# Each subtraction that makes the low part of a weight chunk goes to GpSimd in two halves

## The chip, the cores and the metric

The kernel runs on one core of one Trainium2 chip. The time is device microseconds (us) of one execution, the median of the runs shown. Engines are named as in the profile: PE (TensorE matmul) and PEld (its weight loads), DVE (VectorE), ACT (ScalarE), POOL (GpSimd), SP (SyncE, which issues most DMAs).

## The reference, cut to what matters

Two layers of a diffusion backbone over 256 latent and 256 context tokens, width 1024, all in float32. A layer is a SwiGLU feed-forward (FFN), a mixer with three branches (gated linear attention, 2-D neighbourhood attention, grouped-query attention) that are gated and merged, and a second FFN. After the mixer of layer 1 only the 256 latent tokens go on.

```python
for l in range(DEPTH):
    ...
    x = x + 0.5 * g1 * swiglu(modulate(rms_norm(x, norm_g[l, 0]), sh1, sc1), ffn_w_in[l, 0], ffn_w_out[l, 0])
    h = h + 0.5 * cg1 * swiglu(modulate(rms_norm(h, norm_g[l, 0]), ch1, cs1), ffn_w_in[l, 0], ffn_w_out[l, 0])
    y, yc = token_mixer(...)
    x = x + g2 * y
    x = x + 0.5 * g3 * swiglu(modulate(rms_norm(x, norm_g[l, 2]), sh3, sc3), ffn_w_in[l, 1], ffn_w_out[l, 1])
    if need_ctx:
        ...
```

## The kernel before

The large products keep float32 accuracy with three passes of the faster fp32r form. Each operand is split into a high part (the value rounded to fp32r) and a low part (the value less its high part), and `mm3` issues high x high, high x low and low x high into one PSUM bank.

Weights come in 504 chunks. A chunk is 128 partitions by 1024 floats at most: four row blocks of 128 input rows by 256 columns (names `up`, `dn` and `pf` on PE), or two row blocks by 512 columns (`pt`); 16 `dn` chunks have two row blocks of 256 columns. The first index of a chunk's tile, `a` in the code, counts the row blocks. A chunk goes through four steps: a DMA into `w_raw` (three buffers), ACT's rounding copy into `w_hi`, POOL's subtraction `w_raw - w_hi` into `w_lo`, and the matmuls. `w_hi` and `w_lo` have three buffers each, so the split of a chunk starts only when PE has ended the chunk three places earlier. On a full chunk PE runs 24 matmuls for each stretch of tokens that it handles at a time (512 or 256 columns).

The order of all engines' instructions is fixed when the program is built. `Program.run` walks through the chunks; the main matmuls are issued directly, and side work (norms, attention heads, the modulation products `mod_acc`, the splits of chunks) stands in generators which are resumed after each few matmuls and which issue an instruction when a planner's clock (`Clock`) says that its inputs are there. The planner's durations decide the order only. For POOL it counts 0.1 us and 2.35 ns an element for each instruction, and it keeps the times of a tile's pieces apart.

At the start of a FFN or a mixer the two first column blocks are handled together (the `both` case in `ffn`, `proj_f2` in the mixer): one chunk is kept until its partner is there, and PE then goes through both, 256 tokens after 256 tokens. The activations `u_hi` and `u_lo` that these products read are made just then by a chain of DVE instructions (`norm_chain`).

In `splitter` the subtraction is one instruction of the whole chunk, except for four chunks at the very start (`halves`, set in `ffn` for the first FFN's first column blocks), where it is two instructions over half the row blocks each.

Of the kernel before, what the change touches and what calls it, by code (L numbers as in the profile page):

```python
# [49 lines left out]
def r32(ap):  # L50
    return ap.bitcast(F32R)
# [149 lines left out]
class Program:  # L201
# [76 lines left out]
        while self.urgent:  # L278
            self.round_or_stall()

    def chunk(self, src, a, b, fn, split=True, halves=False, kept=False):

        self.items.append(("c", (src, a, b, split, halves), fn))
        if kept:
            self.kept.add(sum(it[0] == "c" for it in self.items))

# [68 lines left out]
    def run(self):  # L355
        specs = [it[1] for it in self.items if it[0] == "c"]
        raws, parts, ended = {}, {}, {}
        state = {"loaded": 0, "ci": 0}

        def load(n):  # L360
            while state["loaded"] < min(len(specs), n):
                j = state["loaded"]
                src, a, b = specs[j][:3]
                raw = self.rpool.tile([P, a, b], F32, name="w_raw", tag="r", padded_shape=[P, 1024 // b, b])
                old = raws.get(j - RAW_BUFS)
                if old is not None:
                    self.clock.floor[raw.name] = self.clock.read.get(old.name, 0.0)
                self.clock.dma(raw)
                self.nc.sync.dma_start(raw, src)
                raws[j] = raw  # L370
                state["loaded"] += 1

        def splitter():
            for j, (src, a, b, do, halves) in enumerate(specs):
                while j > state["ci"] + SPLIT_AHEAD or (j >= SPLIT_BUFS and j - SPLIT_BUFS not in ended):
                    yield None
                load(j + 1)
                hi = self.wpool.tile([P, a, b], F32, name="w_hi", tag="w", padded_shape=[P, 1024 // b, b])
                lo = self.wpool.tile([P, a, b], F32, name="w_lo", tag="w", padded_shape=[P, 1024 // b, b])
                self.clock.floor[hi.name] = self.clock.floor[lo.name] = ended.get(j - SPLIT_BUFS, 0.0)  # L380
                raw = raws[j]
                yield from self.gact.copy(r32(hi), raw)
                h = a // 2 if halves else a
                for s in range(0, a, h):
                    yield from self.ggp.tensor_tensor(r32(lo[:, s : s + h]), raw[:, s : s + h], hi[:, s : s + h], op=ALU.subtract)
                parts[j] = (r32(hi), r32(lo))
                load(j + 1 + RAW_BUFS)
                if self.force:
                    yield None

        self.load = load
        split = splitter()

        def advance(g):

            self.first = True
            self._resume(g)
            self.first = False

        work = self.round  # L400

        def round_with_splits():
            n = self.clock.count
            advance(split)
            w = list(self.wakes)
            more = work()
            self.wakes += w
            return more or self.clock.count > n

        self.round = round_with_splits  # L410
        for kind, _, fn in self.items:
            if kind == "f":
                self.flush()
                fn()
                continue
            ci = state["ci"]
            load(ci + 1)
            self.force = True
            while ci not in parts:
                advance(split)  # L420
            self.force = False
            fn(parts.pop(ci))
            if ci + 1 not in self.kept:
                ended[ci] = self.clock.now
            if ci in self.kept:
                ended[ci - 1] = self.clock.now
            state["ci"] = ci + 1
        self.flush()
        assert not self.sides, list(self.sides)
# [3 lines left out]
def tile_backbone(ctx: ExitStack, tc: tile.TileContext, I: dict, out: bass.AP):  # L433
# [12 lines left out]
    prog = Program(nc, rpool, wpool)  # L446
# [22 lines left out]
    def acc_bank(name):  # L469
        t = psa.tile([P, 512], F32, name=name, tag="a")  # L470
        accs.append(t)
        if len(accs) > 4:
            clock.floor[t.name] = clock.read.get(accs[-5].name, 0.0)
        return t
# [183 lines left out]
    def lead(k, r):  # L658

        if k < 6 and k % 2 == 0:  # L660
            first_mm(k // 2 + 1, r)
        elif k % 2 and k < 7 and r == 0:
            first_u(k // 2 + 1)
# [167 lines left out]
    def need(r, k):  # L831

        while st["done"][r] <= k:
            prog.round_or_stall()
# [55 lines left out]
    def wsrc(w, k0, k1, c0, c1):  # L890
        return w[k0 * P : k1 * P, c0:c1].rearrange("(k p) n -> p k n", p=P)

    def ffn(l, i, which, n, square, ahead=(), lead=None):

        w_up, w_dn = I["ffn_w_in"][l, which], I["ffn_w_out"][l, which]
# [3 lines left out]
        def up(mp, part, kh, both=False):  # L899


            def fn(w):
                if both and part == 0:
                    hold["w"] = w
                    return
                ws = [(0, hold["w"]), (1, w)] if both else [(part, w)]
                for p, _ in ws:
                    if kh == 0:
                        hold[p] = [acc_bank("up") for _ in range(2)]
                parts = [slice(r, r + LAT) for r in range(0, n, LAT)] if both else [slice(0, n)]  # L910
                order = [(kk, r) for r in range(len(parts)) for kk in range(4)]
                for kk, r in sorted(order) if lead and both else order:
                    k, c = 4 * kh + kk, parts[r]
                    if lead and both:
                        lead(k, r)
                    elif both:
                        need(r, k)
                    uh, ul = st["u"][k]
                    for p, (wh, wl) in ws:
                        for m in range(2):  # L920
                            s = slice(m * P, (m + 1) * P)
                            mm3(hold[p][m][:, c], (wh[:, kk, s], wl[:, kk, s]), (uh[:, c], ul[:, c]), k + r == 0, k == KT - 1 and c is parts[-1])
                        prog.tick(0.25 * (c.stop - c.start) / NT)
                if kh:
                    for p, _ in ws:
                        evac(mp, p)

            return fn
# [93 lines left out]
        for a, b in ((0, 12), (12, NH)):  # L1022
            for mp in range(a // 2, b // 2):
                both = mp == 0
                order = [(0, 0), (1, 0), (0, 1), (1, 1)] if mp == 0 else [(0, 0), (0, 1), (1, 0), (1, 1)]
                for j, (part, kh) in enumerate(order):
                    c0 = part * D_FF + mp * 256
                    prog.chunk(wsrc(w_up, 4 * kh, 4 * kh + 4, c0, c0 + 256), 4, 256, up(mp, part, kh, both), halves=lead and both, kept=both and part == 0)
                if both and lead:
                    prog.call(lambda: load_vectors(1))  # L1030
                    prog.call(lambda: mod_side(st["mod_blocks"]))
            if a == 0:
                mod_need(l, 24 * i + 16, 24 * i + 24)
                prog.call(gates)
                if late_vectors:
                    prog.call(late_vectors.pop())
            for fp in range(4):
                if a and fp == 0:
                    if square:
                        mod_need(square[0], 24 * square[1], 24 * square[1] + 16)  # L1040
                    mod_prefetch(("ahead", l, i), ahead)
                if a and fp == 3 and square:
                    ks = [(a, a + 2), (a + 2, a + 6), (a + 6, b)]
                    for (k0, k1), (fn, kept) in zip(ks, last_down(ks)):
                        prog.chunk(wsrc(w_dn, k0, k1, fp * 256, fp * 256 + 256), k1 - k0, 256, fn, kept=kept)
                    continue
                for k0 in range(a, b, 4):
                    k1 = min(k0 + 4, b)
                    prog.chunk(
                        wsrc(w_dn, k0, k1, fp * 256, fp * 256 + 256),  # L1050
                        k1 - k0,
                        256,
                        down(fp, k0, k1, k0 == a, k1 == b, b == NH),
                    )
# [1016 lines left out]
```

## Time and profile before

| | |
|---|---|
| median of 3 runs | 2881.67 us (2880.91 to 2881.89) |
| profiled execution | 2878.06 us, span 2876.3 us |
| PE busy | 2777.6 us, 97% of the span |
| DVE, ACT, POOL busy | 58%, 35%, 45% |
| mean granted clock of PE | 0.985 |

The span runs from the first to the last instruction; the execution's own time has some 1.8 us around it. An engine's busy time includes time in which an instruction has started and is held up.

### The profile page before, as it was taken

The page shows a single profiled execution, that of the slowest core. Times are in us where ns is not written, and L with a number is a line of the kernel's source. Part 1 is how long each engine was busy: PE and PEld are TensorE (multiplying, and loading weights), DVE is VectorE, ACT ScalarE, POOL GpSimd, SP SyncE. Part 2 cuts the span into 40 slices and gives each one's busy share as a digit, 9 for nine tenths or more (in the row PEclk, how much of TensorE's full clock was granted, in tenths as well). Part 3 has the DMA queues.
Part 4 walks back from the last instruction along what each step waited for, and adds up shares of the span by engine and source line. Part 5 has one row for each costly group of instructions (what it writes and reads, how often), then busy time and mean ns, then how long its engine had stood idle before and what let it go on. Part 6 is the DMA issues. An engine that isn't in the chain of part 4 may idle for free.

```text
span 2876.3 us, 39661 instructions
## 1 busy us (share of the span) xinstructions
PE 2777.6 (97%) x15547; PEld 2330.8 (81%) x15547; DVE 1662.6 (58%) x2970; ACT 1007.2 (35%) x1598; POOL 1288.1 (45%) x585
## 2 busy tenths in 40 slices
PE   8999998999999999999999989999999998999999
PEld 6888877778777888877888878888787777899899
DVE  5654566768765675675545575212555659757522
ACT  2222223433444344322312212222244345454443
POOL 3444433224333442434444434444433455657687
PEclk9999999999999999999999989999999999999999
DMA  6444443224222222433444434333323334435554
GB/s 228 159 147 133 151 129 107 77 81 131 80 73 78 81 74 62 161 125 109 144 143 139 161 102 146 101 96 99 110 70 85 95 100 115 132 103 180 172 184 155
DMA packets 295647, 346.46 MB, mean 120 GB/s; under 512 B 15541, under 2 KB 238806, under 8 KB 295460
## 3 DMA queue, kind: packets, MB, share of 16 engines
q1 hardware_dynamic: 294964, 343.58, 38.0%
q8 instruction: 122, 2.00, 0.3%
q14 instruction: 65, 0.53, 0.1%
q0 software_dynamic: 320, 0.28, 0.0%
q10 hardware_dynamic: 176, 0.07, 0.0%
HBM read 342.83 MB, written 1.05 MB: 120 GB/s over the span
## 4 chain that ended last, share of the span: by engine, by line
PE 86%; DVE 8%; issue 4%; POOL 1%; DMA 0%; ACT 0%; SPq 0%; DVEq 0%; POOLq 0%; ACTq 0%
PE up L169 28%; PE pf L169 17%; PE dn L169 15%; PE pt L169 15%; PE a_s L196 2%; PE a_t L196 2%; PE n_o L196 1%; POOL w_lo L196 1%; PE g_o L196 1%; PE q_o L196 1%; PE g_U L196 1%; PE a_qk L196 1%; DVE rs_a L196 1%; DVE z L169 1%; DVE a_p L196 1%
## 5 line engine op out<-in xcount | busy, mean ns | idle before, releaser
L196 POOL TENSOR_TENSOR w_lo<-w_raw,w_hi 128x1024 fp32r<-128x1024 f32 (+1 forms) x508 | 1228.2, 2422 | 1538.3 <-ACT w_hi L196 1480.3
L196 ACT CAST w_hi<-w_raw 128x1024 fp32r<-128x1024 f32 (+1 forms) x504 | 520.6, 1036 | 993.5 <-issue 311.9
L169 PE MATMUL up<-u_hi,w_lo 128*128 128x512 f32 (+1 forms) x1504 | 534.3, 355 | 16.1 <-POOL w_lo L196 16.0
L169 PE MATMUL up<-u_hi,w_hi 128*128 128x512 f32 (+1 forms) x1504 | 536.5, 357 | 6.4 <-DVE u_hi L196 4.1
L169 PE MATMUL up<-u_lo,w_hi 128*128 128x512 f32 (+1 forms) x1504 | 534.3, 355 | 5.0 <-DVE u_lo L196 4.8
L196 DVE SCALAR_TENSOR_TENSOR mod_acc<-mod_w,scv,mod_acc 128x512 f32<-128x512 f32 x364 | 372.7, 1070 | 57.3 <-DMA mod_w<-w_mod 57.0
L169 PE MATMUL dn<-ff_h,w_hi 128*128 128x512 f32 (+1 forms) x1528 | 396.8, 349 | 0.0
L169 PEld LDWEIGHTS up<-u_hi,w_hi 128*128 128x128 f32 x1504 | 290.9, 193 | 56.0 <-issue 11.0
L169 PEld LDWEIGHTS up<-u_hi,w_lo 128*128 128x128 f32 x1504 | 290.9, 193 | 54.9 <-POOL w_lo L196 17.1
L169 PEld LDWEIGHTS up<-u_lo,w_hi 128*128 128x128 f32 x1504 | 290.7, 193 | 43.4 <-DVE u_lo L196 6.0
L169 PEld LDWEIGHTS dn<-ff_h,w_hi 128*128 128x128 f32 x1528 | 267.6, 189 | 38.9 <-ACT w_hi L196 1.7
L169 PE MATMUL dn<-ff_h,w_lo 128*128 128x512 f32 (+1 forms) x764 | 265.9, 348 | 0.0
L169 PE MATMUL pt<-w_hi,u_hi 128*128 128x512 f32 x640 | 261.8, 409 | 0.0
L169 PE MATMUL pf<-u_hi,w_hi 128*128 128x256 f32 (+1 forms) x736 | 250.9, 341 | 10.3 <-DVE u_hi L196 7.0
L169 PE MATMUL pt<-w_hi,u_lo 128*128 128x512 f32 x640 | 250.8, 392 | 0.0
L169 PE MATMUL pt<-w_lo,u_hi 128*128 128x512 f32 x640 | 250.5, 391 | 0.0
L169 PE MATMUL pf<-u_hi,w_lo 128*128 128x256 f32 (+1 forms) x736 | 239.9, 326 | 8.7 <-POOL w_lo L196 8.7
L169 PE MATMUL pf<-u_lo,w_hi 128*128 128x256 f32 (+1 forms) x736 | 240.3, 327 | 5.8 <-DVE u_lo L196 5.7
L169 DVE TENSOR_TENSOR ff_h<-ff_a,up 128x512 f32<-128x512 f32 (+1 forms) x88 | 53.3, 620 | 317.0 <-PE up L169 278.7
L169 PE MATMUL pf<-y,w_hi 128*128 128x512 f32 (+1 forms) x768 | 195.6, 345 | 3.1 <-DVE y L196 1.9
L169 PEld LDWEIGHTS pf<-u_hi,w_hi 128*128 128x128 f32 x736 | 143.7, 195 | 30.9 <-issue 9.4
L169 DVE SCALAR_TENSOR_TENSOR x<-dn,ff_g,x 128x256 f32<-128x256 f32 x112 | 47.1, 478 | 202.0 <-PE dn L169 201.8
(227 smaller groups left out, 4043.0 us busy)
## 6 DMA issues: line engine op xcount, KB each, us to landing
w_raw<-ffn_w_in SPq DMA_DIRECT2D x176, 512.0 KB
w_raw<-w_in SPq DMA_DIRECT2D x168, 512.0 KB
mod_w<-w_mod SPq DMA_DIRECT2D x288, 256.0 KB
w_raw<-ffn_w_out SPq DMA_DIRECT2D x80, 512.0 KB
w_raw<-w_branch SPq DMA_DIRECT2D x48, 512.0 KB
w_raw<-w_out SPq DMA_DIRECT2D x16, 512.0 KB
w_raw<-ffn_w_out SPq DMA_DIRECT2D x16, 256.0 KB
n_rel<-nat_rpb SPq DMA_DIRECT2D x32, 109.5 KB
```

The costliest lines, as they stand in the source:

```text
L169: return real(*args, **kw)
L196: return real(*args, **kw)
```

## The change

The flag `halves` goes, and every chunk's subtraction is issued as two instructions, each over half of the row blocks.

```diff
-    def chunk(self, src, a, b, fn, split=True, halves=False, kept=False):
+    def chunk(self, src, a, b, fn, split=True, kept=False):
 
-        self.items.append(("c", (src, a, b, split, halves), fn))
+        self.items.append(("c", (src, a, b, split), fn))
...
-            for j, (src, a, b, do, halves) in enumerate(specs):
+            for j, (src, a, b, do) in enumerate(specs):
...
-                h = a // 2 if halves else a
+                h = a // 2
                 for s in range(0, a, h):
                     yield from self.ggp.tensor_tensor(r32(lo[:, s : s + h]), raw[:, s : s + h], hi[:, s : s + h], op=ALU.subtract)
...
-                    prog.chunk(wsrc(w_up, 4 * kh, 4 * kh + 4, c0, c0 + 256), 4, 256, up(mp, part, kh, both), halves=lead and both, kept=both and part == 0)
+                    prog.chunk(wsrc(w_up, 4 * kh, 4 * kh + 4, c0, c0 + 256), 4, 256, up(mp, part, kh, both), kept=both and part == 0)
```

On POOL, in the first FFN and at the start of the next norm (a number behind x counts equal rows in a row; rows with - are of before, rows with + of the change):

```order
-L196 TENSOR_TENSOR w_lo<-w_raw,w_hi 128x512 x8
-L196 TENSOR_TENSOR w_lo<-w_raw,w_hi 128x1024 x54
-L196 TENSOR_TENSOR w_lo<-w_raw,w_hi 128x512
-L196 TENSOR_TENSOR w_lo<-w_raw,w_hi 128x1024 x2
-L196 TENSOR_TENSOR w_lo<-w_raw,w_hi 128x512
-L196 TENSOR_TENSOR w_lo<-w_raw,w_hi 128x1024 x2
+L196 TENSOR_TENSOR w_lo<-w_raw,w_hi 128x512 x116
+L196 TENSOR_TENSOR w_lo<-w_raw,w_hi 128x256 x2
+L196 TENSOR_TENSOR w_lo<-w_raw,w_hi 128x512 x4
+L196 TENSOR_TENSOR w_lo<-w_raw,w_hi 128x256 x2
+L196 TENSOR_TENSOR w_lo<-w_raw,w_hi 128x512 x4
```

The first eight rows of 512 elements stay; each subtraction of 1024 elements became two of 512, and each of 512 (a `dn` chunk of two row blocks) two of 256.

On PE, in the first products of layer 0's second FFN, 24 matmuls behind the one that waits for the first piece of the second chunk pair's `w_lo`; what a row waits for stands in brackets. Before:

```order
L169 MATMUL up<-u_hi,w_lo 128x256
L169 MATMUL up<-u_hi,w_hi 128x256
L169 MATMUL up<-u_lo,w_hi 128x256
L169 MATMUL up<-u_hi,w_lo 128x256
L169 MATMUL up<-u_hi,w_hi 128x256
```

The same place with the change:

```order
L169 MATMUL up<-u_lo,w_hi 128x256
L169 MATMUL up<-u_hi,w_lo 128x256 [waits Pool_49]
L169 MATMUL up<-u_hi,w_hi 128x256
L169 MATMUL up<-u_lo,w_hi 128x256
L169 MATMUL up<-u_hi,w_lo 128x256
```

The order of the matmuls is the same; the first one that reads the second half of the tile has a wait for POOL of its own. In the FFNs and norms this is all that changes on PE.

On DVE, early in the attention heads of layer 1's mixer (`a_p` is a head's softmax, `a_mx` its maxima, `gg_w` belongs to the first branch's gate):

```order
 L196 TENSOR_SCALAR rs_v<-h_ss 128x8
 L196 ISA a_s,a_mx<-a_s,n_tab,a_mx 128x256
 L196 ISA a_mx 128x1
-L196 TENSOR_SCALAR a_p<-a_p,a_rs 128x512
-L196 RECIPROCAL a_rs<-a_sm 128x1
-L196 TENSOR_SCALAR a_mx<-a_mx 128x1
+L196 TENSOR_REDUCE h_ss<-h_sq 128x4
+L196 TENSOR_SCALAR a_mx<-a_mx 128x1
+L196 SCALAR_TENSOR_TENSOR gg_w<-gg_t,pf 128x256 x2
+L196 RECIPROCAL a_rs<-a_sm 128x1
+L196 TENSOR_SCALAR a_mx<-a_mx 128x1
+L196 TENSOR_REDUCE a_mx<-a_s 128x1
```

Here the planner lets other work go ahead of the softmax's scaling. Such shifts of side work stand in both mixers; with tile numbers left out, PE's order differs at some 90 places, all but the last two of them in the mixers.

## Rows read from the trace of the kernel before

**Rows 1.** The page's head and its busy times by engine.
```profile
span 2876.3 us, 39661 instructions
...
PE 2777.6 (97%) x15547; PEld 2330.8 (81%) x15547; DVE 1662.6 (58%) x2970; ACT 1007.2 (35%) x1598; POOL 1288.1 (45%) x585
```

**Rows 2.** What PE waited for: us in total, times, longest.
```profile
PE up L169 <- POOL w_lo L196: 16.0, 4, 6.8
PE pf L169 <- POOL w_lo L196: 8.7, 3, 4.8
PE a_t L196 <- DVE a_p L196: 7.8, 6, 4.4
...
PE pf L169 <- DVE u_lo L196: 5.7, 6, 2.4
```

**Rows 3.** Matmuls that waited, in order of time: start, us, idle before.
```profile
47.52 0.39 PE L169 MATMUL up<-u_hi,w_lo 128*128 128x256 f32 x1 [1.13 <-POOL w_lo L196]
...
499.54 0.39 PE L169 MATMUL pf<-u_hi,w_lo 128*128 128x256 f32 x1 [1.93 <-POOL w_lo L196]
...
1307.54 0.58 PE L169 MATMUL up<-u_hi,w_lo 128*128 128x256 f32 x1 [6.76 <-POOL w_lo L196]
...
2686.10 0.39 PE L169 MATMUL up<-u_hi,w_lo 128*128 128x256 f32 x1 [1.82 <-POOL w_lo L196]
```

**Rows 4.** The tile w_lo on POOL: duration in ns, least, median and longest.
```profile
L196 POOL TENSOR_TENSOR w_lo<-w_raw,w_hi x508: 1258/2396/7294, 20.1 to 2865.7; 128x1024 fp32r<-128x1024 f32 x158, 128x512 fp32r<-128x512 f32 x12
```

**Rows 5.** POOL's groups by shape: us in all, mean ns of one.
```profile
L196 POOL TENSOR_TENSOR w_lo<-w_raw,w_hi 128x1024 fp32r<-128x1024 f32 x484 | 1194.9, 2472 | 1488.2 <-ACT w_hi L196 1430.3 <-PE g_oT L196 30.3 <-PE q_o L196 8.0
L196 POOL TENSOR_TENSOR w_lo<-w_raw,w_hi 128x512 fp32r<-128x512 f32 x24 | 33.7, 1413 | 50.1 <-ACT w_hi L196 50.0
```

**Rows 6.** POOL in order of time, rows that follow each other merged: start, us.
```profile
20.15 4.94 POOL L196 TENSOR_TENSOR w_lo<-w_raw,w_hi 128x512 fp32r<-128x512 f32 x4 [13.76 <-ACT w_hi L196]
...
497.13 4.70 POOL L196 TENSOR_TENSOR w_lo<-w_raw,w_hi 128x1024 fp32r<-128x1024 f32 x2 [13.67 <-ACT w_hi L196]
```

**Rows 7.** POOL and DVE at two FFN starts, in order of time.
```profile
1300.19 9.62 POOL L196 TENSOR_TENSOR w_lo<-w_raw,w_hi 128x1024 fp32r<-128x1024 f32 x2 [22.41 <-ACT w_hi L196]
...
1302.55 2.74 DVE L196 SCALAR_TENSOR_TENSOR mod_acc<-mod_w,scv,mod_acc 128x512 f32<-128x512 f32 x4
...
1695.44 9.16 POOL L196 TENSOR_TENSOR w_lo<-w_raw,w_hi 128x1024 fp32r<-128x1024 f32 x2 [20.89 <-ACT w_hi L196]
...
1696.02 4.06 DVE L196 SCALAR_TENSOR_TENSOR mod_acc<-mod_w,scv,mod_acc 128x512 f32<-128x512 f32 x6
```

**Rows 8.** POOL and DVE at a norm and among attention heads.
```profile
1669.84 2.36 POOL L196 TENSOR_TENSOR w_lo<-w_raw,w_hi 128x1024 fp32r<-128x1024 f32 x1 [11.38 <-ACT w_hi L196]
...
1670.27 2.08 DVE L196 TENSOR_SCALAR u_hi<-n_t,mod 128x256 fp32r<-128x256 f32 x1
...
1675.47 0.34 DVE L196 TENSOR_SCALAR u_hi<-n_t,mod 128x256 fp32r<-128x256 f32 x1
...
2457.76 2.58 POOL L196 TENSOR_TENSOR w_lo<-w_raw,w_hi 128x1024 fp32r<-128x1024 f32 x1 [2.50 <-ACT w_hi L196]
...
2458.05 2.57 DVE L196 TENSOR_SCALAR a_p<-a_p,a_rs 128x512 f32<-128x512 f32 x1
...
2463.12 0.47 DVE L196 TENSOR_SCALAR a_p<-a_p,a_rs 128x512 f32<-128x512 f32 x1
```

**Rows 9.** Stretches: us, busy by engine, granted clock (PEclk), DMA share, GB/s.
```profile
500.90:504.30 3.40, 3.40 (x19) 3.40 (x19) 3.40 (x9) 0.00 (x0) 0.92 (x1) 0.53 0.76 213
...
2139.30:2142.70 3.40, 3.40 (x19) 3.40 (x18) 3.37 (x8) 0.00 (x0) 1.10 (x1) 0.53 0.78 213
...
2683.00:2690.00 7.00, 5.18 (x43) 4.98 (x42) 3.03 (x4) 2.84 (x3) 4.71 (x2) 1.00 0.31 84
...
2376.00:2670.00 294.00, 275.07 (x2106) 251.02 (x2104) 221.78 (x432) 148.57 (x274) 177.25 (x80) 0.97 0.45 137
...
2694.00:2876.00 182.00, 178.13 (x1481) 177.30 (x1479) 48.77 (x61) 76.04 (x103) 145.32 (x63) 1.00 0.56 174
```

**Rows 10.** PE's longest wait in layer 1's attention heads, 2376 to 2670 us.
```profile
PE a_t L196 <- DVE a_p L196: 7.2, 5, 4.4
```

## The prediction

> **What bounds the kernel now.** I read the busy times first. PE is busy 2777.6 of 2876.3 us [rows 1], so what can be won is its 98.7 us of idle time and the stretches in which its clock is low. POOL is busy 45% of the span: it bounds nothing by its total, and what counts is when single pieces of its work are ready.
>
> Next came the list of what PE waited for. The longest entry is POOL's `w_lo`: 16.0 us in four waits of `up` and 8.7 us in three waits of `pf`, 24.7 us together [rows 2]. The timeline shows them one by one. Of the seven, the first (1.13 us at 47.5) comes from a chunk that goes in halves already. The other six stand at the starts of mixers and FFNs, from 1.82 to 6.76 us long [rows 3], and sum to 24.7 - 1.1 = 23.6 us.
>
> Then I looked at why a subtraction is late. It takes 2.40 us as a rule (the median) and at worst 7.29 [rows 4]. The worst one starts at 1300.19. DVE's run of `mod_acc` ends at 1302.55 + 2.74 = 1305.29, and the subtraction at 1300.19 + 7.29 = 1307.48, so 2.2 us of it come after DVE's last instruction; PE goes on at 1307.54 [rows 3, 7]. The pair at 1695 shows the same: DVE's run ends at 1700.08. POOL and DVE hold each other up. The other direction shows too: a `u_hi` of DVE, 0.34 us when free, takes 2.08 when it starts behind a subtraction, and an `a_p` takes 2.57 where it needs 0.47 [rows 8]. DVE is then late for PE: 7.8 us of waits for `a_p`, 5.7 for `u_lo` [rows 2].
>
> **The change part by part.**
>
> *The pieces.* A whole subtraction takes 2.40 us; a piece of 512 elements takes 1.26 at the least [rows 4]. The mean of the 24 such pieces is 1.41 [rows 5], which includes pieces held up by DVE. Four pieces in a row took 4.94 us and two wholes 4.70 [rows 6], so that splitting a chunk costs POOL (4.94 - 4.70) / 2 = 0.12 us. I take 1.27 for the first piece. The second ends 0.12 us later than the whole would have.
>
> *Waits for `w_lo`.* In all six waits PE needs only the first half to go on; the order shows the wait for the second half 24 matmuls further. DVE's run ahead of the subtraction stays as it is, so what shrinks is the part behind it: each of the six waits shortens by 2.40 - 1.27 = 1.13 us, together **6.8 us**, and each is longer than this [rows 3]. The second half comes 1.2 us after the first. In between PE has the 24 matmuls of 256 columns; in the last FFN, where all have 256 columns, 1481 of them fill 178.1 us [rows 9], 0.12 us each, so they cover 2.9 us. Should DVE get in between the pieces, a late second half would cost what exceeds this. I set the bounds at 6.0 (0.2 us lost in each of four places) and 6.8.
>
> *The clock.* After the waits of 1.9 and 2.0 us at 499 and 2138, the granted clock is 0.53 for 3.4 us, that is about 1.2 of the 2.4 GHz; around the wait of 1.82 us at 2686 it stays at 1.00 [rows 3, 9]. Such a stretch does 0.53 x 3.4 = 1.8 us worth of work and costs 1.6. With waits of 0.8 instead of 1.9 us both stretches might go: 0 to 3.2 us; the row at 2686 is nearest, but other waits stand near the two, and I take one, **1.6 us**. The longer waits, 4.8 to 6.8 us, stay above 3.6, and I count nothing there.
>
> *DVE behind POOL at the norms.* With pieces, a DVE instruction that starts behind a subtraction can go when the piece is over. The `u_hi` at 1670.27 would end at about 1669.84 + 1.27 + 0.34 = 1671.45 and not at 1672.35 [rows 8]. But the instructions behind it depend on it, and each may meet the next piece, so a chain of several gains no more than one piece, 0 to 1.1 us. There are two such norms where PE waits behind it (the one of 1670 and the one ahead of layer 1's mixer, whose waits for `u_lo` are among those of [rows 2]): 0 to 2.2 us, and nearer to the upper end by the row of 1670, **1.5 us**.
>
> *DVE behind POOL in the attention heads.* In layer 1's heads PE waits five times for `a_p`, 7.2 us in all [rows 10]. Each held-up `a_p` could end up to 1.1 us earlier (2.40 - 1.27): 0 to 5.5 us. Since some of these start in the second half of a subtraction already, I take **3.0**.
>
> *What it costs.* The 504 chunks had 508 subtractions and get 1008. The 0.12 us a chunk, 60 us on POOL, lie beside PE: in the last FFN, where chunks are shortest, POOL is busy 145.3 of 182 us and 63 subtractions would grow by 7.6 to 153 [rows 9]. Were that cover gone, POOL would set the pace there and the cost be 7.6 us at most. PE's new waits fall on matmuls whose data are long there; ACT and SP get more waits on POOL's and each other's counts ahead of their instructions, and both have idle time. I count 0.
>
> *The moved side work.* In the mixers the planner puts side work elsewhere. Layer 0's mixer leaves PE nearly no idle time; in layer 1's heads PE idles 294.0 - 275.1 = 18.9 us [rows 9]. A shift there may remove or add a wait as long as the longest, 4.4 us [rows 10]. I take 0, with 4.4 to either side.
>
> **The sum.** 6.8 + 1.6 + 1.5 + 3.0 = 12.9 us. Against the profiled execution's 2878.06 (span 2876.3) this gives 2865.2; the median of the runs shown is 3.6 us above that execution, so the forecast is 2881.67 - 12.9 = 2868.8. At best 6.8 + 3.2 + 2.2 + 5.5 + 4.4 = 22.1 us are gained (2859.6), at worst 6.0 - 4.4 = 1.6 (2880.1).
>
> **The rivals.**
>
> *No change that shows.* Only the six waits shrink, DVE's chains are held up by two pieces as by one whole, and the moved side work takes back 4.4 us: 2881.67 - 6.8 + 4.4 = 2879.3. For it speaks that a dependent chain meets both pieces; against it that held-up single instructions (`a_p`) are what PE waits for.
>
> *Slower: DVE takes the gap between the pieces.* The rows of 1300 show that a run of DVE instructions keeps POOL out for 5 us. If such a run gets in after the first piece, the second piece is late by its length, up to 4.06 us [rows 7]. It decides where PE needs the second half soon: in `pt` chunks three matmuls after the first. If the forecast's gains are there too, it takes more than 12.9 + 5.8 = 18.7 us of such waits to end slower, five late pieces of 4 us; with eight and none of the gains but the six waits the time is 2881.67 - 6.8 + 8 x 4.0 = 2907. Against it: before, no `pt` matmul and no matmul in layer 1's heads is in the list of waits for `w_lo`, so POOL runs ahead there. The Trainium skill (SBUF — State Buffer, section "Who interferes with whom") says that a GpSimd instruction that reads SBUF and a VectorE one with two SBUF inputs never share: whoever issues first has the port for its whole instruction, and the other blocks fully. By that rule alone, pieces let a held-up DVE instruction go earlier (the third and fourth term) and open this gap as well (the 2907 us). The trace agrees with it in both directions, with 7.29 us for a subtraction and 2.57 for an `a_p`.
>
> *More than forecast.* DVE's held-up time falls everywhere and the heads of layer 1 lose half of their 18.9 us of idle time: 6.8 + 3.2 + 2.2 + 9.4 = 21.6 us, 2860.
>
> **Chances.** Forecast (2862 to 2875.9) 0.58, more than that 0.10, no change 0.22, slower 0.10. A measurement of this kernel tells 0.2%, 5.8 us, from no change. So faster 0.68, same 0.22, slower 0.10. The range of 2858 to 2882 leaves out the slower case and the ends of the others.
>
> **What would show it.** Right: the waits for `w_lo` on PE fall from 24.7 to about 18 us, the wait near 1307 to 5.6, the rows near 499 and 2138 to 0.8; a first piece lands 1.27 us after its start, the `a_p` group's mean falls, POOL's busy time rises by about 60 us and PE's wait list has no `pt` row for `w_lo`. Wrong: waits on a second piece; a wait near 1307 that has not moved (DVE's run longer, or the wait for a whole tile still); new waits in the heads of layer 1 longer than those that went; or low-clock stretches where none were.

## The result, and the profile after

The changed kernel takes 2864.59 us (median of 4 runs, 2862.87 to 2866.51) where the kernel before, run beside it, takes 2881.29 (2878.27 to 2881.89): a ratio of 0.9944 [0.9927, 0.9962], 16.7 us less. The forecast was 2868.8, 12.9 us less. The total came out near it, but the experiments below show that two of its terms were far off in opposite directions.

The page's head and busy times of the kernel after, which answer to [rows 1]:

```profile
span 2863.8 us, 40613 instructions
...
PE 2775.4 (97%) x15547; PEld 2330.4 (81%) x15547; DVE 1582.1 (55%) x2968; ACT 1010.4 (35%) x1600; POOL 1425.2 (50%) x1085
```

The span is 12.5 us shorter than that of the execution profiled before. PE runs the same 15547 matmuls. Its idle time fell from 98.7 to 2863.8 - 2775.4 = 88.4 us, by 10.3; its busy time fell by 2.2, and since the matmuls are the same, a change of their busy time is above all a change of the granted clock. DVE's busy time fell by 80.5 us with nearly the same work (two of its 2970 instructions went to ACT). POOL's rose by 137.1.

A trace is one execution. The kernel before ran 26 times beside the experiments below, and its mean granted clock went from 0.982 to 0.985, its time from 2877.3 to 2886.9 us. So a difference of a few us in PE's busy time between two traces shows little by itself.

What PE waited for in the kernel after (us in total, times, longest), against [rows 2]:

```profile
PE a_s L196 <- ACT a_p L196: 13.6, 4, 6.5
PE up L169 <- POOL w_lo L196: 13.1, 4, 5.7
...
PE a_t L196 <- DVE a_p L196: 5.5, 4, 3.8
...
PE pf L169 <- POOL w_lo L196: 4.3, 3, 2.2
...
PE pf L169 <- DVE u_lo L196: 3.7, 6, 0.9
```

The waits for `w_lo` went from 24.7 to 17.4 us, and there is still none in a `pt` chunk. The waits for DVE's `a_p` and `u_lo` are shorter. The first row has grown: PE's `a_s` waits 13.6 us for ACT's `a_p`; before, the same entry had 5.3 us, in two waits, the longest 3.2.

The matmuls that waited for `w_lo`, in order of time (start, us, and in brackets the idle time before), against [rows 3]:

```profile
494.71 0.39 PE L169 MATMUL pf<-u_hi,w_lo 128*128 128x256 f32 x1 [1.13 <-POOL w_lo L196]
...
1303.81 0.58 PE L169 MATMUL up<-u_hi,w_lo 128*128 128x256 f32 x1 [5.69 <-POOL w_lo L196]
...
2673.95 0.39 PE L169 MATMUL up<-u_hi,w_lo 128*128 128x256 f32 x1 [0.83 <-POOL w_lo L196]
```

These are the places of 499, 1307 and 2686 in [rows 3], with 0.80, 1.07 and 0.99 us less. All waits for `w_lo` stand at first pieces; no matmul waits for a second one.

POOL's groups by shape in the kernel after (us in all, mean ns of one), against [rows 5]:

```profile
L196 POOL TENSOR_TENSOR w_lo<-w_raw,w_hi 128x512 fp32r<-128x512 f32 x976 | 1339.7, 1396 | 1365.9 <-ACT w_hi L196 1308.3 <-PE g_oT L196 15.3 <-DMA w_raw<-ffn_w_in 12.9
...
L196 POOL TENSOR_TENSOR w_lo<-w_raw,w_hi 128x256 fp32r<-128x256 f32 x32 | 26.4, 846 | 17.9 <-ACT w_hi L196 17.9
```

Two pieces take 2 x 1.396 = 2.79 us on the mean, where a whole took 2.47 [rows 5]: 0.32 us more and not 0.12. Four pieces in a row took only 4.94 us [rows 6], so the surplus is, at least for the most part, time in which pieces are held up. PE waits for a held piece only at the starts listed under `w_lo` above.

### The profile page after: what moved, and what is told of

Same layout as the page of the kernel before. It is cut to its first block, busy times and chain, and to the rows that moved or that the text cites. A ratio compares the mean times of both kernels' runs of the same rounds, so it can differ in the third digit from the quotient of the medians.

```text
span 2863.8 us, 40613 instructions
## 1 busy us (share of the span) xinstructions
PE 2775.4 (97%) x15547; PEld 2330.4 (81%) x15547; DVE 1582.1 (55%) x2968; ACT 1010.4 (35%) x1600; POOL 1425.2 (50%) x1085
## 5 line engine op out<-in xcount | busy, mean ns | idle before, releaser
L196 POOL TENSOR_TENSOR w_lo<-w_raw,w_hi 128x512 fp32r<-128x512 f32 (+1 forms) x1008 | 1365.7, 1378 | 1383.8 <-ACT w_hi L196 1326.2
L196 DVE SCALAR_TENSOR_TENSOR mod_acc<-mod_w,scv,mod_acc 128x512 f32<-128x512 f32 x364 | 337.5, 972 | 82.0 <-DMA mod_w<-w_mod 81.9
L169 PEld LDWEIGHTS dn<-ff_h,w_lo 128*128 128x128 f32 x764 | 144.6, 189 | 18.4
```

The lines of the kernel that those rows point to most:

```text
L169: return real(*args, **kw)
L196: return real(*args, **kw)
```

## The experiments

The changed kernel differs from the one before in two things: POOL's instructions are shorter, and the planner, which sees the pieces, deals the mixers' side work out anew. The first batch takes them apart. In its first kernel a stub lets the planner count one whole subtraction, while two pieces are issued. The order of PE, ACT, DVE and SP is then that of the kernel before, instruction by instruction.

```diff
+class Planned:
+
+    def tensor_tensor(self, *args, **kw):
+        return None
...
                 h = a // 2
+                p = a // 2 if j < 4 else a
+                for s in range(0, a, p):
+                    yield from self.gplan.tensor_tensor(r32(lo[:, s : s + p]), raw[:, s : s + p], hi[:, s : s + p], op=ALU.subtract)
                 for s in range(0, a, h):
-                    yield from self.ggp.tensor_tensor(r32(lo[:, s : s + h]), raw[:, s : s + h], hi[:, s : s + h], op=ALU.subtract)
+                    self.nc.gpsimd.tensor_tensor(r32(lo[:, s : s + h]), raw[:, s : s + h], hi[:, s : s + h], op=ALU.subtract)
...
+    prog.gplan = Gated(prog, "POOL", Planned())
```

`h` sets the pieces that are issued and `p` those that the planner counts; the other kernels differ from this one in one line each.

**Pieces in the order of before.** Expected: 

> Every subtraction in two pieces, but the planner still counts one whole, so that all other engines keep the order of before. Theory one (the pieces themselves shorten waits): the whole gain of 16.7 us stays, 2864 to 2868 us. Rival (the mixers' new order gives all that is not a wait for w_lo): only the 7.3 us by which PE's waits for w_lo fell, about 2874 us.

Measured: 2849.65 us, ratio 0.9892 [0.9879, 0.9906], 31.2 us less than before. Both expectations were wrong. In the old order the pieces are worth nearly twice what the change brought.

**Whole subtractions in the order of after**: `h = a if j >= 4 else a // 2`, `p = a // 2`. Expected: 

> Whole subtractions, but in the order that the planner makes when it counts two pieces: the order of the change on all other engines without the pieces. Theory one: as before within 4 us, 2877 to 2885 us. Rival (the new order gains): 2881.3 less some 9 us, about 2872 us.

Measured: 2893.0 us, ratio 1.0043 [1.0030, 1.0055], 12.1 us more than before. Both expectations were wrong: the order alone makes the kernel slower. With pieces it costs 2864.6 - 2849.7 = 14.9 us. So the 16.7 us are some 31 gained by the pieces less some 15 lost by the order.

**Pieces for the seven late chunks alone** (the fourth ones of the paired blocks, at the starts of mixers and FFNs, at which the six waits of [rows 3] and a seventh start stand), in the old order:

```diff
-                h = a // 2
+                h = a // 2 if j < 4 or j in (71, 79, 187, 255, 323, 331, 439) else a
```

Expected: 

> The order of before; two pieces only for the first four chunks, as before, and for seven more: the fourth chunk of each pair of column blocks that is handled together (six of them are those that PE waited for). Theory one: the six waits shorten by 1.13 us each and one stretch of low clock goes, 2881.3 - 6.8 - 1.6 = 2873 us. Rival (the gain comes from DVE being released earlier everywhere, the waits for w_lo only move): 2880 us.

Measured: 2872.62 us, ratio 0.9971 [0.9959, 0.9982], 8.3 us less. The forecast's first two terms, waits and clock, are 6.8 + 1.6 = 8.4 us. The agreement is looser than it looks: the ratio's interval is 5 to 12 us, and in the profiled execution the waits for `w_lo` fell by 5.4 us (24.7 to 19.3), while PE's busy time, 2777.6 before, did not fall:

```profile
PE 2778.1 (97%) x15547; PEld 2331.4 (81%) x15547; DVE 1666.9 (58%) x2970; ACT 1007.3 (35%) x1598; POOL 1287.8 (45%) x592
```

**Pieces for all chunks but those seven**: `h = a if j in (71, 79, 187, 255, 323, 331, 439) else a // 2`. Expected: 

> The order of before; two pieces for every chunk but those seven. Theory one: what is left of the gain when the six waits stay, that is DVE's instructions being released earlier: 2881.3 - (16.7 - 8.4) = 2873 us, with the waits for w_lo on PE at 24 us as before. Rival (all of the gain is in the six waits and in the order): 2881 us.

Measured: 2857.53 us, ratio 0.9919 [0.9906, 0.9933], 23.3 us less. Both expectations were too high. The two parts add up: 8.3 + 23.3 = 31.6 against 31.2. No wait for `w_lo` is shortened in this kernel, so the 23 us come from somewhere else. The forecast had 1.5 + 3.0 = 4.5 us for it.

Where the time goes shows in the stages. Layer 1's mixer, from its first product to the first one of the last FFN, takes 611 us before, 596 with pieces in the old order and 610 after. These are the windows of that stage in the three kernels, in this order (length, busy by engine, granted clock, DMA share, GB/s):

```profile
2065.00:2676.00 611.00, 578.33 (x3736) 493.62 (x3732) 408.46 (x868) 271.01 (x473) 310.70 (x150) 0.98 0.38 113
```

```profile
2052.00:2648.00 596.00, 574.41 (x3740) 492.49 (x3732) 385.67 (x866) 271.53 (x473) 339.64 (x268) 0.98 0.39 116
```

```profile
2055.00:2665.00 610.00, 578.30 (x3740) 494.70 (x3732) 393.20 (x869) 272.12 (x472) 340.75 (x268) 0.97 0.38 113
```

Of the 15 us that the pieces win there in the old order, 32.7 - 21.6 = 11.1 are idle time of PE and 578.3 - 574.4 = 3.9 are matmuls at a higher clock. With the new order both are lost again: 31.7 us idle, 578.3 busy.

Waits of PE in that stage, before (beside those for `a_p` in [rows 10]) and then with pieces in the old order:

```profile
PE pf L169 <- DVE u_lo L196: 4.4, 4, 2.4
PE a_t L196 <- DVE a_pt L196: 2.6, 1, 2.6
```

```profile
PE a_s L196 <- ACT a_p L196: 5.1, 2, 3.1
PE a_t L196 <- DVE a_p L196: 2.5, 1, 2.5
PE pf L169 <- DVE u_lo L196: 2.4, 4, 0.9
```

The waits for `a_p` fell by 4.7 us and those for `u_lo` by 2.0; the one for `a_pt` is gone. In this stage DVE runs the same instructions in the same order, and they take 22.5 us less: 8.2 of these are `z`, 4.6 `a_p`, 3.9 `y` and 2.4 `gg_w`. What holds the instruction up shows at one place of the program, an `a_p` that starts behind a subtraction. Before, and then with pieces in the old order (POOL and DVE in order of time):

```profile
2418.23 2.39 POOL L196 TENSOR_TENSOR w_lo<-w_raw,w_hi 128x1024 fp32r<-128x1024 f32 x1 [7.34 <-PE n_o L196]
2418.53 2.37 DVE L196 TENSOR_SCALAR a_p<-a_p,a_rs 128x512 f32<-128x512 f32 x1
```

```profile
2397.82 2.71 POOL L394 TENSOR_TENSOR w_lo<-w_raw,w_hi 128x512 fp32r<-128x512 f32 x2 [2.51 <-ACT w_hi L196]
2398.11 1.28 DVE L196 TENSOR_SCALAR a_p<-a_p,a_rs 128x512 f32<-128x512 f32 x1
```

The `a_p` ends 1.1 us sooner, and the next DVE instruction goes in ahead of POOL's second piece's end.

The stage is also where the new order loses. This is how PE comes to wait 5.07 us there in the kernel after (in order of time):

```profile
2433.37 2.35 DVE L196 TENSOR_TENSOR q_sw<-q_raw,cossin 128x128 f32<-128x128 f32 x2
...
2434.28 6.04 POOL L196 TENSOR_TENSOR w_lo<-w_raw,w_hi 128x512 fp32r<-128x512 f32 x4
...
2435.64 1.78 DVE L196 TENSOR_TENSOR q_rot<-q_raw,cossin 128x512 f32<-128x512 f32 x1
...
2437.35 1.25 DVE L196 SCALAR_TENSOR_TENSOR rs_y<-rs_a,rs_y 128x8 f32<-128x8 f32 x1
...
2439.13 1.22 DVE L196 TENSOR_TENSOR rs_a<-rs_y 128x8 f32<-128x8 f32 x1
...
2442.89 0.69 ACT L196 ACTIVATE a_p<-a_s,a_mx 128x512 f32<-128x512 f32 x1 [7.29 <-DVE a_mx L196]
...
2443.72 0.79 PE L196 MATMUL a_s<-a,a 64*128 64x512 f32 x1 [5.07 <-ACT a_p L196]
```

DVE works on a rotation (`q_sw`, `q_rot`) and a norm (`rs_a`, `rs_y`), held up by the subtractions, while the head's maxima `a_mx` stand behind them; ACT waits 7.29 us for these and PE 5.07 for ACT. The clock falls with it, and once more near a wait of 3.8 us for `a_p` at 2602. Two stretches of the kernel after:

```profile
2440.90:2451.10 10.20, 6.54 (x25) 5.28 (x26) 9.86 (x32) 2.50 (x6) 2.87 (x3) 0.51 0.26 79
2601.30:2608.10 6.80, 5.45 (x22) 4.64 (x23) 2.72 (x7) 2.14 (x7) 0.00 (x0) 0.52 0.24 77
```

With pieces in the old order there are 3.4 us near the first of these places (at 2437.8) and none near the second.

**Second batch: where, how much further, and why the order.** Pieces in layer 1's mixer alone, old order: `h = a // 2 if j < 4 or 320 <= j < 436 else a`. Expected: 

> Pieces for the chunks of layer 1's mixer alone (and the first four), in the order of before. The landmarks of the run with pieces everywhere in the old order put 15.0 of its 31.2 us into that mixer. Theory (the gain there is made there, by DVE instructions of the heads that a shorter subtraction holds up less): 15 us less than before, 2866, and the matmuls' steps at 2412, 2420, 2461, 2590 and 2650 of before shrink as they did with pieces everywhere. Rival (the heads gain because the work ahead of them has run earlier, norms and FFNs included): the gain in the mixer falls below 5 us, 2876 or more.

Measured: 2865.48 us, ratio 0.9939 [0.9925, 0.9952], 16.2 us less than the kernel before in this batch (2881.63). The theory holds: the gain of that mixer is made in that mixer. In the trace, of an execution 3.5 us slower than the median, PE is 1.0 us behind the kernel before when the stage starts and 10.7 ahead when it ends.

**The planner counts pieces in layer 1's mixer alone**, pieces everywhere: `p = a // 2 if j < 4 or 320 <= j < 436 else a`. Expected: 

> Pieces everywhere; the planner counts pieces only in layer 1's mixer (and for the first four chunks) and wholes elsewhere. Theory (the new order costs its 12 to 15 us in layer 1's mixer): 2849.7 + 13 = 2863, lost between 2430 and 2620 of the span. Rival (the cost sits in what layer 0's mixer hands on, or needs all of the new order): 2852 or less.

Measured: 2864.62 us, ratio 0.9939 [0.9926, 0.9951]. That is 15.0 us above pieces in the old order: the whole cost of the new order lies in this one stage, in which PE's order is that of the kernel after, matmul by matmul. Its wait list has the row of after again:

```profile
PE a_s L196 <- ACT a_p L196: 13.5, 4, 6.5
PE a_t L196 <- DVE a_p L196: 4.9, 3, 3.8
```

**The planner counts wholes that are 0.1 us longer**, pieces everywhere: `return 0.2 + n * 0.00235` in the planner's cost of POOL. Expected: 

> Pieces everywhere; the planner counts a whole for each chunk, but 0.1 us longer (0.2 us and 2.35 ns an element), as long as two pieces together. Theory (any shift of the planner's POOL clock deals the heads' side work out anew, and the order of before was a lucky or tuned one): an order unlike both, 2853 to 2866. Rival (the order is spoilt by the times of single pieces, which let the splits and what follows them go ahead): with no such times the order stays as good as that of before, 2848 to 2852.

Measured: 2862.38 us, ratio 0.9933 [0.9921, 0.9946], 12.7 us above pieces in the old order. It has no times of single pieces, and its order is unlike both others. Its waits for `a_p` are near those of the old order, and another one has come:

```profile
PE pf L169 <- DVE z L169: 7.6, 1, 7.6
...
PE a_s L196 <- ACT a_p L196: 6.2, 2, 5.1
```

So what costs is not a property of the pieces. Of three orders that the planner made of slightly different numbers, the one of before is the best by 13 to 15 us; whether it was once chosen for that, no run here shows.

**Pieces of one row block**, four of 256 elements in most chunks, old order: `h = 1`. Expected: 

> In the order of before, each subtraction in as many pieces as it has row blocks: four of 256 elements in the FFNs and most of the mixers, two of 512 in pt chunks. Theory (what pays is how long one POOL instruction holds DVE and PE's first data): a piece of 256 takes about 0.70 us instead of 1.27, so the six waits shrink by another 0.57 us each, 3.4 us, and DVE's gain of 23 us, which came from 1.13 us less per piece, grows by about half, 11 us: 2849.7 - 15 = 2835. Rival (DVE takes the gaps and the last piece is late, and POOL's 0.12 us a cut, 0.24 us more a chunk, adds up): 2850 or more, with waits on the third or fourth piece.

Measured: 2855.38 us, ratio 0.9906 [0.9892, 0.9919], 5.7 us above halves, which ran in the first batch. The gain that was expected is not there, and the reason is not the rival's. The waits for `w_lo` fell from 19.4 to 14.8 us, somewhat more than expected, with none on a later piece. Up to the end of layer 1's mixer the kernel is 29.2 us ahead of before, halves 27.6, so outside the waits the shorter pieces bring nothing more there. In the last FFN 7.1 us are lost. POOL and DVE there, in order of time:

```profile
2679.37 21.65 POOL L394 TENSOR_TENSOR w_lo<-w_raw,w_hi 128x256 fp32r<-128x256 f32 x31
```

```profile
2683.20 0.78 DVE L169 TENSOR_TENSOR ff_h<-ff_a,up 128x256 f32<-128x256 f32 x2 [7.89 <-PE up L169]
2684.09 17.54 DVE L196 TENSOR_TENSOR ff_h<-ff_h,ff_h 128x256 fp32r<-128x256 f32 x2
```

POOL runs 31 pieces in 21.65 us, 0.70 us each, without a gap. A DVE `ff_h`, 0.41 us at the least, takes 17.2 us and ends 0.3 us after this run of pieces. A second one (9.34 us, at 2722.9) lets PE wait 5.3 us. Every other `ff_h` of this FFN took 0.41 to 0.96 us, also in the middle of such runs.

**Blocks in the last FFN alone, halves elsewhere**: `h = 1 if j >= 436 else a // 2`. Expected: 

> Old order, halves up to the end of layer 1's mixer, blocks of one row block in the last FFN alone. Theory (a run of short POOL pieces without a gap starves DVE in this stage whatever came before): 2849.7 + 7.1 + 1.3 = 2858, with an ff_h held for over 5 us and a wait of PE for it. Rival (it was how blocks in the mixer had shifted the start of the stage): 2850, no such row.

Measured: 2857.93 us, ratio 0.9915 [0.9900, 0.9929]. The time is the theory's, 6.4 us above the kernel of the same batch that has halves in nearly all of this FFN (2851.51, the last one below). Three `ff_h` took over 14 us. One of them:

```profile
2669.69 19.58 POOL L394 TENSOR_TENSOR w_lo<-w_raw,w_hi 128x256 fp32r<-128x256 f32 x28
```

```profile
2675.14 14.74 DVE L196 TENSOR_TENSOR ff_h<-ff_h,ff_h 128x256 fp32r<-128x256 f32 x2
```

PE's listed waits in the last FFN are only 2.4 us for `ff_h` in this profile, less than the 5 that were expected. And a run of pieces without a gap does not hold every `ff_h`. In the same FFN two of them, one behind the other, took 1.31 us inside a longer run:

```profile
2719.74 31.15 POOL L394 TENSOR_TENSOR w_lo<-w_raw,w_hi 128x256 fp32r<-128x256 f32 x44 [2.74 <-ACT w_hi L196]
```

```profile
2727.32 1.31 DVE L196 TENSOR_TENSOR ff_h<-ff_h,ff_h 128x256 fp32r<-128x256 f32 x2 [1.23 <-ACT ff_h L196]
```

**Blocks up to the last FFN, halves in it**: `h = 1 if j < 436 else a // 2`. Expected: 

> Old order; pieces of one row block up to the end of layer 1's mixer, halves in the last FFN. With blocks everywhere the landmarks stood 29.2 us ahead of before at the start of the last FFN (halves: 27.6) and lost 7.1 us inside it, where one DVE instruction of 0.41 us is held for 17.2 us while POOL runs 31 pieces without a gap. Theory (only this starving of DVE spoils the blocks): 2855.4 - 7.1 - 1.3 = 2847, a little under halves everywhere. Rival (the loss moves with the work, or the blocks lose elsewhere too): 2851 or more.

Measured: 2846.95 us, ratio 0.9875 [0.9860, 0.9890]: the lowest time of all, as the theory had it, 34 us less than before and 17.6 less than the change. Against halves everywhere, measured in another batch, it is 2.7 us, and the two intervals overlap, so it is not shown that blocks outside the last FFN gain anything. They cost nothing there, not even where POOL runs without a gap, as at the end of layer 1's mixer:

```profile
2588.79 49.09 POOL L394 TENSOR_TENSOR w_lo<-w_raw,w_hi 128x256 fp32r<-128x256 f32 x60
```

No DVE instruction beside these 60 pieces took over 1.31 us, and none of the whole kernel over 1.83.

**Blocks for the seven late chunks, halves elsewhere**: `h = 1 if j in (71, 79, 187, 255, 323, 331, 439) else a // 2`. Expected: 

> Old order, halves everywhere, but the seven late fourth chunks (71, 79, 187, 255, 323, 331, 439) in four pieces. Theory (PE needs only the first piece, and a first piece of 256 elements ends 0.57 us before one of 512): six waits shrink by 0.57 us each, 2849.7 - 3.4 = 2846. Rival (the second piece is then what PE waits for, or DVE takes the gaps): 2849.7 or more.

Measured: 2851.51 us, ratio 0.9892 [0.9876, 0.9909], the same ratio as halves everywhere. The waits for `w_lo` fell by 4.2 us, more than the 3.4 expected, and PE's idle time from 79.8 to 76.8. But PE's busy time rose, for the same matmuls:

```profile
PE 2773.0 (97%) x15547; PEld 2329.2 (82%) x15547; DVE 1579.6 (55%) x2970; ACT 1008.6 (35%) x1598; POOL 1431.0 (50%) x1099
```

```profile
PE 2767.6 (97%) x15547; PEld 2324.9 (82%) x15547; DVE 1582.0 (56%) x2970; ACT 1007.9 (35%) x1598; POOL 1430.4 (50%) x1085
```

The first is this kernel, the second halves in the old order: 5.4 us more of PE busy against 3.0 us less of idle time. But these are two single executions: the profiled one of this kernel had a mean clock of 0.987, and its three others, at the same time to 1 us, had the 0.988 to 0.989 of halves in the old order. The theory was right on the waits. The expected 3.4 us did not show in the time; the ratio's interval, some 9 us wide, has room for them, so this stays open.

## Why the prediction was right, and where its steps were not

*Waits for `w_lo`, 6.8 us: right in the sum, not wait by wait.* The six waits fell from 23.6 to 16.3 us in the kernel after, by 0.8 to 2.6 us each. With pieces in the old order they fell to 18.2: five by 0.99 to 1.08 us, close to the 1.13 of the forecast, and the one near 1702 by 0.08. Before, and then with pieces in the old order:

```profile
1702.33 0.58 PE L169 MATMUL up<-u_hi,w_lo 128*128 128x256 f32 x1 [6.30 <-POOL w_lo L196]
```

```profile
1688.26 4.06 DVE L196 SCALAR_TENSOR_TENSOR mod_acc<-mod_w,scv,mod_acc 128x512 f32<-128x512 f32 x6
...
1693.50 0.58 PE L169 MATMUL up<-u_hi,w_lo 128*128 128x256 f32 x1 [6.22 <-POOL w_lo L394]
```

There the step "DVE's run ahead of the subtraction stays as it is" failed. Before, DVE's run of `mod_acc` began as PE's wait began (1696.0); in the old order with pieces it began 1.0 us later than the wait (1687.3), and the first piece ended 1.1 us after that run, so that what the piece saved went into the later start. PE goes on at the first piece in every kernel with pieces, and no later piece makes it wait.

*The clock, 1.6 us: near in the kernel after, but the link to the waits is not shown.* Both stretches that the forecast named went in the kernel after; the granted clock at these places is now 1.00:

```profile
494.70:498.10 3.40, 3.39 (x28) 3.39 (x29) 3.40 (x4) 0.00 (x0) 3.40 (x3) 1.00 0.18 28
2125.30:2128.70 3.40, 3.31 (x26) 3.11 (x26) 3.40 (x3) 0.44 (x1) 3.40 (x3) 1.00 0.30 64
```

With pieces in the old order, the second is back after the same wait of 0.91 us:

```profile
2123.70:2127.10 3.40, 3.40 (x19) 3.40 (x18) 3.37 (x5) 0.00 (x0) 2.75 (x3) 0.54 0.53 154
```

And the kernel with pieces in layer 1's mixer alone, which runs as before up to there, had the same wait of 1.93 us near 500 and full clock behind it, 31 matmuls in 3.4 us, where the kernel before had 0.53 and 19 [rows 9]:

```profile
500.90:504.30 3.40, 3.40 (x31) 3.40 (x31) 3.40 (x4) 0.04 (x1) 1.92 (x1) 1.00 0.62 169
```

So the length of one wait does not tell whether the clock falls, and that the shorter waits took the two stretches away is not shown. Over the kernel PE's busy time fell by 2.2 us with the new order, near the forecast's 1.6, and by 10.0 with pieces in the old order (2777.6 to 2767.6). That last gain is no accident of one trace: all executions with it had a mean clock of 0.988 or 0.989, against 0.982 to 0.985 of the kernel before beside them. The forecast looked at two stretches near two waits and left out all the others.

*DVE behind POOL, 1.5 + 3.0 us: the mechanism right, the size wrong by a factor of five.* Pieces that touch no late chunk bring 23.3 us. The step that failed is the one that counted what PE was seen to wait for: "In layer 1's heads PE waits five times for `a_p`, 7.2 us in all." The `a_p` waits of the heads gave 4.7 us, not far above the 3.0 taken for them. But in the same stage a wait of 2.6 us for `a_pt`, 2.0 us of waits for `u_lo` and 3.9 us of low clock went too, and the step left out all of DVE's other work behind a subtraction, `z`, `y` and `gg_w` above all. Layer 1's mixer gave 15.0 us in all. Which microsecond goes back to which instruction, and where in the other stages the rest of the 23.3 us arises, no run takes apart. The rival "more than forecast" (21.6 us) had the mechanism nearer to its size.

*The moved side work, 0 with 4.4 us to either side: wrong.* It cost 14.9 us with pieces and 12.1 without, all in layer 1's mixer. The step that failed is the bound: "A shift there may remove or add a wait as long as the longest, 4.4 us." The order differs at some 90 places. At the start of the heads two waits, 3.2 and 2.1 us before, became one of 6.5, with 10.2 us of low clock in either kernel. Two of 5.1 and 3.8 came, where with pieces in the old order there is one of 2.5 and none; beside these two the low clock is new (10.2 us for 3.4, and 6.8 for none).

*POOL's cost, hidden: right on the time, wrong on the size.* POOL's busy time rose by 137 us and not by 60, because two pieces took 0.32 us more than a whole on the mean, where 0.12 was taken. In the last FFN nothing came of it with halves. With blocks that stage lost time, and not by POOL's total, as the forecast had it; what the traces show there is DVE kept out.

*The rival "slower: DVE takes the gap between the pieces"*: no later piece made PE wait in any run. POOL's first pieces were still held by DVE's runs, as the whole subtractions had been (6.7 us near 1687 with pieces in the old order); what came new, with blocks, was DVE kept out.

The sum was near by luck: the DVE terms were some 19 us too small, the term of the order some 15 too good, and the two errors nearly cancelled.

## What to carry to other kernels

Where two engines hold each other up, count the short instruction's gain over everything that starts behind the long one, and not only over the waits that name it. Where a planner's cost model sets the order, a change of the work changes the order too: keep the old order for one run, to tell the two apart, before the change is judged. And try the size of the pieces stage by stage: pieces of one row block lost 7 us in the last FFN, where the other engine was kept out, and lost nothing elsewhere, although POOL ran without gaps in both places.

## What the runs showed of the hardware that was not expected

A DVE instruction can be kept out for the rest of a run of short POOL instructions. An `ff_h` of 0.41 us took 17.2 us beside 31 pieces of 0.70, and 14.4, 14.2 and 14.8 us with blocks in the last FFN alone; each ended 0.3 us after POOL's run of pieces. With halves in the same stage no DVE instruction of the whole kernel took over 2.0 us, though POOL ran 16 of them in 20.9 us there without a gap. The Trainium skill (SBUF — State Buffer, section "Who interferes with whom") says that the second of the two to issue blocks until the first one's instruction is finished. Read as a wait for one instruction, that makes a hold of at most one piece, 0.70 us, and most `ff_h` of that FFN agree (0.41 to 0.97 us). The six long ones of the two kernels, 3.7 to 17.2 us, do not, and the measurement decides: a hold can outlast many instructions of the other side. The other direction showed it already, where one subtraction of 2.40 us was held through a run of several `mod_acc` of 0.5 to 0.75 us each [rows 7]. Which instruction is kept out and which gets in, no run here shows.

Small DVE instructions in a dependent chain are held by one piece each: a norm's `rs_v`, `rs_a` and `rs_y` of two elements, 0.16 us when free, took 0.65 to 0.77 us each beside pieces of 256 elements (with blocks, five of them from 2635.8 on), and 0.16 again when the run of pieces was over. That fits the forecast's argument that a chain of many small steps gains less from shorter pieces than a single late instruction does; no run takes this apart.
